# Projections first as block products, then values with attention, in a hybrid decoder layer

## The chip, the core and the metric

The kernel runs on one core of one Trainium2 chip. The time is the device time of one execution in microseconds (us), and the number compared is the median of several runs. The core has a matrix engine (PE in the profile), a vector engine (DVE), a scalar engine (ACT), a general engine (POOL), and a sync engine (SP), which in this kernel issues the DMA transfers. Each engine works through its own instructions in program order, and waits on semaphores for the others.

## What is computed

```python
h = x * (1 + scale) + shift                      # scale, shift, gate = silu(c) @ w_ada + b_ada
proj = h @ w_in                                  # q k v | g_attn | u B C g_conv | m_attn m_conv
# attention: 3 groups of 4 heads of 128; (window, dilation) = (128,1), (512,4), (2048,16)
s = q . k * 128**-0.5 + bias(distance), causal, window only
o_g = softmax(s) @ v;   lse_g = log of the softmax denominator
o = sum over the 3 groups of softmax(lse)_g * o_g
a_out = (o * silu(g_attn)) @ w_attn_out
# short convolution
z = C * u;  y_conv = conv3_causal(z)
s_out = (B * y_conv * silu(g_conv)) @ w_conv_out
merged = sigmoid(m_attn) * a_out + sigmoid(m_conv) * s_out
out = LayerNorm(alpha * x + (1 + gate) * (merged @ w_o))
```

There are 2048 tokens and 1024 channels, all in float32. To keep the precision, each factor of a big product is split into a rounded part and a remainder ("hi" and "lo"): ScalarE casts the rounded part, VectorE subtracts it to get the remainder, and TensorE runs three matmuls (hi by hi, hi by lo, lo by hi) for each product. Every weight and every activation that goes into such a product costs these two operations.

## The kernel before

Tokens are cut into four chunks of 512. The program has three stages.

The *start* (L180 to L257) computes scale and shift on VectorE while h arrives, and runs the first six query and key units on TensorE as the channels of h arrive. It also builds the twelve bias tables `nb` that attention adds to the scores.

The *attention stage* (L156 to L591) is a list of segments, run by `run_segs` (L156). A segment is one weight unit: a query unit (`qseg`), a key unit (`kseg`), a pair of value units (`vseg`), or a unit of g_attn (`aseg`). A query, key or g_attn unit is a plain product (`gemm`, L140 to L142): 8 channel tiles by 3 matmuls of 128x512, so 24 matmuls. A pair of value units is 4 blocks of 24 matmuls of 128x256 (L186 to L188). The weights of a unit are loaded five segments ahead and split three segments ahead (`wlo`, L103). The parts of attention of a head (scores, transposes, products with the values) are put behind later segments with `after`, so that they alternate with projections. First come the four chunks with groups 1 and 2 (up to about 752 us), whose outputs and softmax statistics go to DRAM (`o_scr`, `st_scr`). Then come the four chunks with group 0 (752 to 1202 us): there `done` (L525 to L557) sends the last statistics through DRAM, works out the weights of the three groups in `al`, writes them to `al_scr`; and `merge` (L559 to L577) loads them broadcast (`ab`), loads the outputs of groups 1 and 2 (`og`), adds the three, and multiplies with silu(g_attn) (`gt`).

The *block products* come last (from L594). Two halves of the tokens and two weights at a time form a product of 2 by 2 blocks, which `products` (L678 to L680) computes with seven block products instead of eight: seven pairs of sums of the blocks (the T rows of the activations, `t_row`: seven splits and four subtractions a row, four rows; and the parts of the weights, `stationary_parts`), then 84 matmuls of 128x512 a step, then sums on VectorE. The stage runs u with C, g_conv with B, m_attn with m_conv (24 steps for each half of the tokens), then the attention output (`w_ao`), the convolution output (`w_co`) for each half, and `w_o` with the LayerNorm.

The places that the prediction speaks of are `gemm` with its users, the merge, `prep` (which loads x, modulates it and splits h for a chunk), and the T rows that each stage of block products begins with.

Of the kernel before, what the change touches and what calls it, by code (L numbers as in the profile page):

```python
# [17 lines left out]
P = 128  # L18
# [5 lines left out]
NH = 4  # L24
# [29 lines left out]
@with_exitstack  # L54
def layer_kernel(ctx: ExitStack, tc: tile.TileContext, x, xm, xn, cvec, wada, bada, w_main, w_v,
                 convw, convb, relb, onehot, w_ao, w_co, w_o, ln_g, ln_b, out):
# [3 lines left out]
    dram = ctx.enter_context(tc.tile_pool(name="dram", bufs=1, space=bass.MemoryType.DRAM))  # L60
    const = ctx.enter_context(tc.tile_pool(name="const", bufs=1))
    stage = ExitStack()
    wp = stage.enter_context(tc.tile_pool(name="wp", bufs=3))
    hp = stage.enter_context(tc.tile_pool(name="hp", bufs=1))
    psum1 = stage.enter_context(tc.tile_pool(name="psum", bufs=1, space=bass.MemoryType.PSUM))

    def bank(tag, bufs):
        return psum1.tile([P, CH], F32, tag=tag, bufs=bufs, name=tag)


    ident = const.tile([P, P], F32, name="ident")
    make_identity(nc, ident)

    def bcast_row(src, n):
        return bass.AP(tensor=src.tensor, offset=src.offset, ap=[[0, P], [1, n]])

    mod = const.tile([P, 3, KT], F32, name="mod")
    badat = const.tile([P, 3, KT], F32, name="badat")
    scp = const.tile([P, KT], F32, name="scp")
    cw = const.tile([P, KT, 4], F32, name="cw")  # L80
    powe = const.tile([P, 1], F32, name="powe")
    halo = const.tile([P, KT, 2], F32, name="halo")


    lagd = dram.tile([3, NH, LAG], F32, name="lagd")
    o_scr = dram.tile([2, NH, NCH, NCH, P, P], F32, name="o_scr")
    st_scr = dram.tile([2, NCH, NH, 4, 2, NCH, 32], F32, name="st_scr")
    st0_scr = dram.tile([NCH, 2, NH * 4, P], F32, name="st0_scr")
    al_scr = dram.tile([NCH, 3, NH * 4, P], F32, name="al_scr")
    om_scr = dram.tile([NCH, P, NH, CH], F32, name="om_scr")  # L90
    y_scr = dram.tile([2, KT, P, 2 * CH], F32, name="y_scr")
    sg_scr = dram.tile([2, 2, KT, P, 2 * CH], F32, name="sg_scr")
    pa_scr = dram.tile([2, KT, P, 2 * CH], F32, name="pa_scr")
    mg_scr = dram.tile([SEQ // P, P, KT, P], F32, name="mg_scr")

    kq = stage.enter_context(tc.tile_pool(name="kq", bufs=1, reuse_waits="tile"))
    nb = [[kq.tile([P, 256 if g < 2 else P], F32, name=f"nb{g}{j}") for j in range(NH)]
          for g in range(3)]


    def split(hi, lo, src):
        S.copy(hi, src)  # L102
        V.tensor_sub(lo, src, hi.bitcast(F32))  # L103
# [6 lines left out]
    def split_unit(raw):  # L110
        hi = wp.tile([P, DM], F32R, name="whi", bufs=3)
        lo = wp.tile([P, DM], F32R, name="wlo", bufs=3)
        split(hi, lo, raw)
        return hi, lo

    def h_pair():
        return (hp.tile([P, CH], F32R, name="hhi", bufs=9), hp.tile([P, CH], F32R, name="hlo", bufs=9))

    def load_x(src, k):
        xs = hp.tile([P, CH], F32, name="xs", bufs=3)  # L120
        SP.dma_start(xs, src[:, k, :])
        return xs

    def modulate(E, xs, k):
        E.tensor_scalar(xs, xs, scp[:, k:k + 1], mod[:, 0, k:k + 1], op0=ALU.mult, op1=ALU.add)
        hi, lo = h_pair()
        split(hi, lo, xs)
        return hi, lo

    def prep(src, store):  # L130
        def pre():
            for k in range(KT):
                store.append(modulate(V, load_x(src, k), k))
        return pre

    def gemm_k(ps, unit, xk, k, n, base=0):
        hi, lo = unit
        xh, xl = xk
        sl = slice((base + k) * P, (base + k + 1) * P)
        PE.matmul(ps, hi[:, sl], xh, start=k == 0, stop=False)  # L140
        PE.matmul(ps, hi[:, sl], xl, start=False, stop=False)  # L141
        PE.matmul(ps, lo[:, sl], xh, start=False, stop=k == n - 1)  # L142

    def gemm(unit, rhs, base=0):
        ps = bank("mm", 3)
        for k, xk in enumerate(rhs):
            gemm_k(ps, unit, xk, k, len(rhs), base)
        return ps
# [35 lines left out]
    def pass3(o, a, b, start, stop):  # L184
# [5 lines left out]
    halos = [(kq.tile([P, P], F32R, name=f"halo_h{j}"), kq.tile([P, P], F32R, name=f"halo_l{j}"))  # L190
             for j in range(NH)]

    def evac_q(g, ps):
        qh = kq.tile([P, CH], F32R, name="qh", bufs=3)
        if g == 2:
            q = qh.bitcast(F32)
            S.activation(classes(q), classes_of(ps), AF.Copy, scale=-QSCALE)
            return q
        ql = kq.tile([P, CH], F32R, name="ql", bufs=3)
        S.activation(qh, ps, AF.Copy, scale=-QSCALE)  # L200
        V.scalar_tensor_tensor(ql, ps, -QSCALE, qh.bitcast(F32), op0=ALU.mult, op1=ALU.subtract)
        return qh, ql

    def evac_k(g, ps, j, c):

        kh = kq.tile([P, P + CH], F32R, name="kh", bufs=3)
        if g == 2:
            k = kh[:, P:].bitcast(F32)
            S.copy(classes(k), classes_of(ps))
            return k  # L210
        kl = kq.tile([P, P + CH], F32R, name="kl", bufs=3)
        split(kh[:, P:], kl[:, P:], ps)
        if g == 0:
            for t, hl in ((kh, halos[j][0]), (kl, halos[j][1])):
                if c > 0:
                    G.tensor_copy(t[:, :P], hl.bitcast(F32))
                if c < NCH - 1:
                    G.tensor_copy(hl, t[:, CH:].bitcast(F32))
        return kh, kl

# [5 lines left out]


    def silu_c(cb, sg):
        SP.dma_start(cb, bcast_row(cvec, DM))
        S.activation(sg, cb, AF.Sigmoid)  # L230
        V.tensor_mul(cb, cb, sg)

    def dot_v(wt, cb, junk, acc):
        for q in range(4):
            sl = slice(q * 256, (q + 1) * 256)
            V.tensor_tensor_reduce(junk, wt[:, sl], cb[:, sl], 1.0, 0.0, ALU.mult, ALU.add,
                                   accum_out=acc[:, q:q + 1])

    def dot_end(m, k, acc):
        V.tensor_reduce(mod[:, m, k:k + 1], acc, axis=AX.X, op=ALU.add)  # L240
        V.tensor_add(mod[:, m, k:k + 1], mod[:, m, k:k + 1], badat[:, m, k:k + 1])

    first_h, first_heads = [], {}
    first_units = [W_Q + NH, W_K + NH, W_Q + NH + 1, W_K + NH + 1, W_Q + NH + 2, W_K + NH + 2]
    with tc.tile_pool(name="ada", bufs=1) as ada:
        cb = ada.tile([P, DM], F32, name="cb")
        silu_c(cb, ada.tile([P, DM], F32, name="prod", bufs=2))
        SP.dma_start(badat, bada)
        flip = ada.tile([P, P], F32, name="flip")
# [783 lines left out]
```

## Time and profile before

| what | us |
|---|---|
| median of 3 runs | 2729.73 (2729.53 to 2733.96) |
| the profiled execution, its own time | 2724.08 |
| its span in the trace | 2722.3 |
| TensorE busy in the span | 2518.6 (93%) |
| VectorE busy | 1684.8 (62%) |
| ScalarE busy | 1002.0 (37%) |
| mean granted clock, as a share of full speed | 0.969 |

The span is the time from the first to the last instruction of the trace. The time of the execution is 1.78 us longer. Busy times are sums over the span, so they say nothing about where an engine waits; for this the rows below go by stretches of the program: start (0 to 100 us), attention with groups 1 and 2 (to 752), with group 0 (to 1202), the last merge (to 1238), the block products of the projections (to 2200), a hand-over, and the output products with the LayerNorm (to 2722).

### The profile page before, as it was taken

To read this page: it belongs to the slowest core of one execution; us is meant where nothing else is said; L and a number is where in the kernel's file an instruction comes from. 1 tells how busy PE (TensorE), PEld (TensorE's weight loads), DVE (VectorE), ACT (ScalarE), POOL (GpSimd) and SP (SyncE) were. 2 spreads that over 40 slices of the span, in tenths; PEclk is the share of its full clock that TensorE was granted. 3 is DMA by queue.
4 is the path that set the end of the run, shared out by engine and by line. 5 is a ranking of instruction groups with operands and counts; after the bars stand their busy time and mean duration, and the time that the engine had idled before them with its cause. 6 is when DMAs were issued, how large, how long until landed. Compare 5 with 4: busy or idle time off the path is not lost.

```text
span 2722.3 us, 31895 instructions
## 1 busy us (share of the span) xinstructions
PE 2518.6 (93%) x12070; PEld 2114.6 (78%) x12070; DVE 1684.8 (62%) x2800; ACT 1002.0 (37%) x1675; POOL 142.3 (5%) x126
## 2 busy tenths in 40 slices
PE   6999999999999999965999999899999988988886
PEld 4898998989988888853888888688888856666665
DVE  8334334243255676747776765777665568788887
ACT  4223333232343434425333343633333343343332
POOL 2000000000000000000000000000000000113123
PEclk9999999999999999986999999999999989998998
DMA  7223233232233553614221233422213247657343
GB/s 261 78 87 116 85 102 108 64 120 78 87 126 100 175 162 122 184 56 162 78 70 62 70 129 135 139 78 70 70 62 116 101 152 266 206 195 238 113 140 104
DMA packets 160302, 331.25 MB, mean 122 GB/s; under 512 B 18727, under 2 KB 70003, under 8 KB 160148
## 3 DMA queue, kind: packets, MB, share of 16 engines
q1 hardware_dynamic: 160148, 329.21, 36.8%
q8 instruction: 94, 1.54, 0.2%
q14 instruction: 60, 0.49, 0.1%
HBM read 265.93 MB, written 63.23 MB: 121 GB/s over the span
## 4 chain that ended last, share of the span: by engine, by line
PE 72%; DVE 12%; DMA 8%; issue 4%; ACT 2%; POOL 1%; SPq 0%; POOLq 0%; DVEq 0%; ACTq 0%
PE pb L678 12%; PE pb L679 12%; PE pb L680 12%; PE mm L140 6%; PE mm L141 6%; PE mm L142 6%; PE mm L188 4%; PE mm L186 4%; PE mm L187 4%; DVE tl L103 2%; DMA og<-o_scr 1%; PE pt L367 1%; DVE w2l L103 1%; DMA xs<-in_xn 1%; DVE hlo L103 1%
## 5 line engine op out<-in xcount | busy, mean ns | idle before, releaser
L678 PE MATMUL pb<-th,w2h 128*128 128x512 f32 x1632 | 650.2, 403 | 105.5 <-ACT th L102 91.3
L679 PE MATMUL pb<-tl,w2h 128*128 128x512 f32 x1632 | 648.2, 399 | 10.9 <-DVE tl L103 10.9
L680 PE MATMUL pb<-th,w2l 128*128 128x512 f32 x1632 | 640.4, 396 | 1.0 <-DVE w2l L103 1.0
L678 PEld LDWEIGHTS pb<-th,w2h 128*128 128x128 f32 x1632 | 312.5, 192 | 201.4 <-ACT th L102 114.8
L103 DVE TENSOR_TENSOR wlo<-raw,whi 128x1024 fp32r<-128x1024 f32 x155 | 189.7, 1224 | 419.3 <-ACT whi L102 410.3
L679 PEld LDWEIGHTS pb<-tl,w2h 128*128 128x128 f32 x1632 | 312.9, 192 | 87.5 <-DVE tl L103 23.9
L680 PEld LDWEIGHTS pb<-th,w2l 128*128 128x128 f32 x1632 | 313.0, 192 | 67.0 <-DVE w2l L103 2.6
L140 PE MATMUL mm<-hhi,whi 128*128 128x512 f32 x856 | 343.0, 401 | 21.2 <-ACT hhi L102 21.2
L142 PE MATMUL mm<-hhi,wlo 128*128 128x512 f32 x856 | 336.2, 393 | 3.9 <-DVE wlo L103 3.9
L141 PE MATMUL mm<-hlo,whi 128*128 128x512 f32 x856 | 336.3, 393 | 1.7 <-DVE hlo L103 1.7
L102 ACT CAST whi<-raw 128x1024 fp32r<-128x1024 f32 x155 | 162.6, 1049 | 446.0 <-issue 184.4
L186 PE MATMUL mm<-whi,hhi 128*128 128x256 f32 x768 | 246.0, 322 | 4.5 <-ACT hhi L102 4.4
L188 PE MATMUL mm<-whi,hlo 128*128 128x256 f32 x768 | 244.8, 323 | 2.0 <-DVE hlo L103 1.8
L187 PE MATMUL mm<-wlo,hhi 128*128 128x256 f32 x768 | 244.5, 321 | 0.0
L102 ACT CAST w2h<-raw 128x1024 fp32r<-128x1024 f32 (+1 forms) x136 | 139.6, 1027 | 275.0 <-PE pb L679 262.0
L103 DVE TENSOR_TENSOR w2l<-raw,w2h 128x1024 fp32r<-128x1024 f32 (+1 forms) x136 | 169.1, 1244 | 110.4 <-ACT w2h L102 110.3
L684 ACT COPY t<-pb 128x512 f32<-128x512 f32 x216 | 125.0, 582 | 232.6 <-PE pb L680 221.3
L140 PEld LDWEIGHTS mm<-hhi,whi 128*128 128x128 f32 x856 | 162.4, 190 | 53.8 <-ACT hhi L102 23.2
L142 PEld LDWEIGHTS mm<-hhi,wlo 128*128 128x128 f32 x856 | 162.1, 189 | 39.4 <-DVE wlo L103 5.0
L186 PEld LDWEIGHTS mm<-whi,hhi 128*128 128x128 f32 x768 | 182.0, 237 | 8.8 <-ACT hhi L102 7.1
L141 PEld LDWEIGHTS mm<-hlo,whi 128*128 128x128 f32 x856 | 162.5, 190 | 33.7 <-DVE hlo L103 2.9
L188 PEld LDWEIGHTS mm<-whi,hlo 128*128 128x128 f32 x768 | 181.2, 237 | 4.7 <-DVE hlo L103 4.0
(197 smaller groups left out, 3513.1 us busy)
## 6 DMA issues: line engine op xcount, KB each, us to landing
raw<-in_w_main SPq DMA_DIRECT2D x208, 512.0 KB
raw<-in_w_v SPq DMA_DIRECT2D x48, 512.0 KB
sg_scr<-big SPq DMA_DIRECT2D x32, 512.0 KB
big<-sg_scr SPq DMA_DIRECT2D x32, 512.0 KB
ab<-al_scr SPq DMA_DIRECT2D x48, 256.0 KB
wt<-in_wada SPq DMA_DIRECT2D x16, 512.0 KB
xs<-in_xm SPq DMA_DIRECT2D x32, 256.0 KB
o_scr<-o SPq DMA_DIRECT2D x32, 256.0 KB
```

Of the source, the lines that this page charges most:

```text
L102: S.copy(hi, src)
L103: V.tensor_sub(lo, src, hi.bitcast(F32))
L140: PE.matmul(ps, hi[:, sl], xh, start=k == 0, stop=False)
L141: PE.matmul(ps, hi[:, sl], xl, start=False, stop=False)
L142: PE.matmul(ps, lo[:, sl], xh, start=False, stop=k == n - 1)
L186: PE.matmul(o, a[0], b[0], start=start, stop=False)
L187: PE.matmul(o, a[0], b[1], start=False, stop=False)
L188: PE.matmul(o, a[1], b[0], start=False, stop=stop)
L678: PE.matmul(bank, hi[:, sl], th, start=first, stop=False, **kw)
L679: PE.matmul(bank, hi[:, sl], tl, start=False, stop=False, **kw)
L680: PE.matmul(bank, lo[:, sl], th, start=False, stop=n == len(rows) - 1, **kw)
L684: S.copy(r, bank)
```

## The change

The query, key and g_attn projections leave the attention stage. They become steps of the block products, and all block products of projections now come first in the program; then attention with only the value projections; then the outputs. In detail:

- The start modulates h straight into T rows of the first half. Its first step (queries of group 1) runs row by row in seven banks (`products_by_row`).
- Queries and keys are 12 steps a half, g_attn 2 steps a half, in place of 24 + 4 plain units for each of four chunks. The results go to `qk_scr` and (as silu) to `ga_scr` in DRAM. For groups 1 and 2 the last sums are written with a stride, in the order of the tokens of a dilated group.
- The bias tables are made between the steps and kept in `nb_scr`; attention loads them back.
- The attention stage has segments of two blocks of values (48 matmuls of 128x256). Queries and keys of a head are loaded from `qk_scr` (`load_qk`) two segments before they are used, cast and split.
- The merge loads `gt` from `ga_scr`, ready for the multiplication.
- The outputs run in the order co of half 0, ao of both halves, co of half 1, w_o.

The core of the diff:

```diff
-                def qseg(i, unit, box=box):
-                    box["q"] = evac_q(g, gemm(unit, h))
-                def kseg(i, unit, j=j, box=box):
-                    attend(i, j, box["q"], evac_k(g, gemm(unit, h), j, c))
-                seg([w_main[W_Q + g * NH + j]], qseg)
-                seg([w_main[W_K + g * NH + j]], kseg)
+    def load_qk(g, j, c, box):
+        n0 = P if g == 0 and c > 0 else 0
+        qr = kq.tile([P, CH], F32, name="qr", bufs=2)
+        kr = kq.tile([P, P + CH], F32, name="kr", bufs=2)
+        SP.dma_start(qr, qk_scr[g * NH + j, :, c * CH:(c + 1) * CH])
+        SP.dma_start(kr[:, P - n0:], qk_scr[12 + g * NH + j, :, c * CH - n0:(c + 1) * CH])
...
+        S.activation(qh, qr, AF.Copy, scale=-QSCALE)
+        V.scalar_tensor_tensor(ql, qr, -QSCALE, qh.bitcast(F32), op0=ALU.mult, op1=ALU.subtract)
+        split(kh[:, P - n0:], kl[:, P - n0:], kr[:, P - n0:])
...
-        after(i + 1, qk)
-        d = 0 if g == 0 and j == NH - 1 else 1
-        after(i + 2 + d, tr)
-        after(i + 3 + d, pv)
+        after(i, qk)
+        after(i + 1, tr)
+        after(i + 2, pv)
...
+            for b0 in (0, 2):
+                i = len(segs)
+                seg([w_v[g, pair, 0], w_v[g, pair, 1]] if b0 == 0 else [],
+                    lambda i, *units, b0=b0, vseg=vseg: vseg(i, *units, b0=b0))
+            for n in range(2):
+                j, at = 2 * pair + n, i + 1 + n
+                qk_box = {}
+                after(at - 2, lambda j=j, qk_box=qk_box: load_qk(g, j, c, qk_box))
...
-            S.activation(ab, gt[j], AF.Sigmoid)
-            V.tensor_mul(gt[j], gt[j], ab)
-            V.tensor_mul(o0[j], o0[j], gt[j])
+            gt = pm.tile([P, CH], F32, name="gt", bufs=2)
+            SP.dma_start(gt, ga_scr[j, :, c * CH:(c + 1) * CH])
+            V.tensor_mul(o0[j], o0[j], gt)
...
-            def aseg(i, unit, h=h, j=j, gt=gt, merge=merge):
-                ps = gemm(unit, h)
+            order = [u + g * NH + j for g in (1, 2, 0) for u in (W_Q, W_K) for j in (0, 2)]
+            for u in order:
+                            if local:
+                                V.tensor_add(m[k][:, at * CH:(at + 1) * CH], r, bank)
+                            else:
+                                V.tensor_add(m[k].rearrange("q (c n a) -> q c n a", c=4, n=2)[:, :, at],
+                                             r.rearrange("q (a c) -> q c a", c=4),
+                                             bank.rearrange("q (a c) -> q c a", c=4))
...
+                if p == 0 and u == W_Q + NH:
+                    todo.append(lambda heads=heads, T=T: products_by_row(S0, T, range(4), *heads()))
+                else:
+                    step(w, w_main[u], w_main[u + 1], CH, use, pre)
+            for j in range(0, NH, 2):
+                def silus(j=j, p=p):
+                            V.tensor_add(o, r, bank)
+                            S.activation(s, o, AF.Sigmoid)
+                            V.tensor_mul(o, o, s)
```

Three places show how instructions move.

SP, the merge of the second chunk of group 0, before. The names are the DRAM buffers of the group weights (`al_scr`), of the outputs of groups 1 and 2 (`o_scr`), of the merged output (`om_scr`), and the weights of the next chunk (`in_w_v`, `in_w_main`).

```order
L557 DMA al_scr<-al 16x3x128
L564 DMA ab<-al_scr 128x512 x3
L107 DMA raw<-in_w_v 128x1024
L564 DMA ab<-al_scr 128x512
L107 DMA raw<-in_w_v 128x1024
L564 DMA ab<-al_scr 128x512
L570 DMA og<-o_scr 128x4x128 x2
L564 DMA ab<-al_scr 128x512
L107 DMA raw<-in_w_main 128x1024
L577 DMA om_scr<-o_7946 128x512
```

The same place after:

```order
L144 DMA kr<-qk_scr 128x640
L392 DMA al_scr<-al 16x3x128
L143 DMA qr<-qk_scr 128x512
L144 DMA kr<-qk_scr 128x640
L399 DMA ab<-al_scr 128x512 x4
L143 DMA qr<-qk_scr 128x512
L399 DMA ab<-al_scr 128x512
L405 DMA og<-o_scr 128x4x128
L399 DMA ab<-al_scr 128x512
L405 DMA og<-o_scr 128x4x128
L399 DMA ab<-al_scr 128x512
L412 DMA om_scr<-o_16116 128x512
```

The weight loads between the broadcasts are gone from this stretch, and loads of queries and keys (`qr`, `kr`) stand in the queue among the loads of the merge.

DVE, the same merge, before (`wlo` is the remainder of a weight unit, `ql` and `kl` those of queries and keys, `o` a head's output, `ab` a broadcast weight, `og` the output of another group):

```order
L103 TENSOR_TENSOR wlo<-raw,whi 128x1024
L103 TENSOR_TENSOR vb<-mm,va 128x256
L567 TENSOR_TENSOR o_7946<-o_7946,ab 128x512
L103 TENSOR_TENSOR wlo<-raw,whi 128x1024
L572 TENSOR_TENSOR ab<-ab,og 128x4x128 x2
L573 TENSOR_TENSOR o_7946<-o_7946,ab 128x512
L103 TENSOR_TENSOR wlo<-raw,whi 128x1024
L573 TENSOR_TENSOR o_7946<-o_7946,ab 128x512
L575 TENSOR_TENSOR gt_8154<-gt_8154,ab 128x512
L201 SCALAR_TENSOR_TENSOR ql<-mm,qh 128x512
L576 TENSOR_TENSOR o_7946<-o_7946,gt_8154 128x512
```

The same merge after (`p,st` are scores with bias and their row statistics):

```order
L156 SCALAR_TENSOR_TENSOR ql<-qr,qh 128x512
L467 TENSOR_TENSOR kl<-kr,kh 128x640
L467 TENSOR_TENSOR vb<-mm,va 128x512
L402 TENSOR_TENSOR o_16116<-o_16116,ab 128x512
L407 TENSOR_TENSOR ab<-ab,og 128x4x128
L194 ISA p,st<-s,nb_10796 128x256
L194 ISA st 128x1
L408 TENSOR_TENSOR o_16116<-o_16116,ab 128x512
L407 TENSOR_TENSOR ab<-ab,og 128x4x128
L402 TENSOR_TENSOR o_16259<-o_16259,ab 128x512
L408 TENSOR_TENSOR o_16116<-o_16116,ab 128x512
L194 ISA p,st<-s,nb_10796 128x256
```

Weight splits stood between the steps of the merge; now scores of the next heads stand there, and `ql` and `kl` are made from loaded tiles (`qr`, `kr`) instead of banks.

DVE, the end of attention, before (`rows` are the statistics of the last head, `al` and `nm` the group weights):

```order
L525 COPY o_10428<-ot 128x512
L471 COPY rows<-pt 32x128
L585 COPY gt_10486<-mm 128x512
L546 TENSOR_TENSOR nm<-al 16x128
L547 TENSOR_TENSOR nm<-nm,al 16x128
L549 TENSOR_TENSOR al<-nm,al 16x128 x3
L551 TENSOR_TENSOR al<-al 16x384
L552 TENSOR_TENSOR nm<-al 16x128
L553 TENSOR_TENSOR nm<-nm,al 16x128
L554 RECIPROCAL nm<-nm 16x128
L556 TENSOR_TENSOR al<-al,nm 16x128 x3
L567 TENSOR_TENSOR o_10076<-o_10076,ab 128x512
```

The same place after (`w2l`, `xs`, `w1l` belong to the first weights of co):

```order
L360 COPY o_17535<-ot 128x512
L467 TENSOR_TENSOR w2l<-raw,w2h 128x1024
L549 TENSOR_TENSOR xs<-raw 128x512
L381 TENSOR_TENSOR nm<-al 16x128
L550 TENSOR_TENSOR xs<-xs,raw 128x512
L382 TENSOR_TENSOR nm<-nm,al 16x128
L554 TENSOR_TENSOR raw<-raw 128x512
L384 TENSOR_TENSOR al<-nm,al 16x128 x3
L467 TENSOR_TENSOR w2l<-xs,w2h 128x1024
L467 TENSOR_TENSOR w2l<-raw,w2h 128x1024
L386 TENSOR_TENSOR al<-al 16x384
```

The weight preparation of the next block products now stands between the steps of the group weights; before, it came behind the merge.

## Rows read from the trace of the kernel before

**Rows 1.** The page: busy time with share, and the chain that ended last.

```profile
PE 2518.6 (93%) x12070; PEld 2114.6 (78%) x12070; DVE 1684.8 (62%) x2800; ACT 1002.0 (37%) x1675; POOL 142.3 (5%) x126
...
PE 72%; DVE 12%; DMA 8%; issue 4%; ACT 2%; POOL 1%; SPq 0%; POOLq 0%; DVEq 0%; ACTq 0%
```

**Rows 2.** Windows by stage: stretch, length, busy us of each engine, clock, DMA.

```profile
core 0: us, PE busy (x) PEld busy (x) DVE busy (x) ACT busy (x) POOL busy (x), PEclk, DMA share, GB/s
0.00:60.00 60.00, 35.71 (x128) 25.73 (x129) 51.63 (x146) 24.50 (x66) 16.52 (x14) 1.00 0.76 274
60.00:100.00 40.00, 36.00 (x248) 31.80 (x247) 20.12 (x35) 10.25 (x18) 0.00 (x0) 1.00 0.42 114
392.00:572.00 180.00, 179.62 (x978) 163.38 (x977) 66.91 (x142) 60.23 (x134) 0.00 (x0) 1.00 0.30 94
752.00:1202.00 450.00, 434.78 (x2504) 380.99 (x2502) 278.45 (x538) 176.95 (x350) 25.49 (x48) 0.98 0.42 132
977.00:1087.00 110.00, 107.13 (x616) 93.96 (x615) 75.76 (x142) 45.24 (x86) 7.77 (x19) 0.98 0.50 156
1202.00:1238.00 36.00, 0.00 (x0) 0.00 (x0) 25.34 (x41) 4.32 (x6) 0.00 (x0) 0.57 0.54 154
1238.00:1290.00 52.00, 32.47 (x99) 21.22 (x100) 42.83 (x65) 32.87 (x46) 0.00 (x0) 0.71 0.50 167
1290.00:1710.00 420.00, 420.00 (x1852) 347.23 (x1851) 285.46 (x430) 155.72 (x188) 0.00 (x0) 1.00 0.27 92
2200.00:2240.00 40.00, 28.52 (x72) 16.52 (x72) 31.38 (x54) 18.19 (x32) 0.00 (x0) 0.70 0.46 151
2240.00:2722.30 482.30, 402.05 (x1614) 307.42 (x1613) 395.39 (x566) 168.99 (x244) 100.29 (x64) 0.93 0.53 181
```

**Rows 3.** Timeline of TensorE: start, duration, engine, line, operation.

```profile
419.10 0.48 PE L140 MATMUL mm<-hhi,whi 128*128 128x512 f32 x1
...
424.65 0.60 PE L367 MATMUL pt<-ident,p 128*128 128x128 f32 x4
...
438.46 0.28 PE L186 MATMUL mm<-whi,hhi 128*128 128x256 f32 x1
...
449.98 0.49 PE L367 MATMUL pt<-ident,p 128*128 128x128 f32 x3
```

**Rows 4.** Groups of VectorE by form, 977 to 1087 us (one chunk of group 0).

```profile
L103 DVE TENSOR_TENSOR wlo<-raw,whi 128x1024 fp32r<-128x1024 f32 x16 | 19.6, 1224 | 15.6 <-ACT whi L102 15.6
...
L575 DVE TENSOR_TENSOR gt<-gt,ab 128x512 f32<-128x512 f32 x4 | 2.9, 726 | 0.0
...
L585 DVE COPY gt<-mm 128x512 f32<-128x512 f32 x4 | 2.8, 689 | 9.7 <-PE mm L142 9.7
```

**Rows 5.** Timeline of VectorE, back to back, in the block products.

```profile
1250.56 1.22 DVE L103 TENSOR_TENSOR w2l<-raw,w2h 128x1024 fp32r<-128x1024 f32 x1
1251.70 0.68 DVE L103 TENSOR_TENSOR w1l<-t,w1h 128x512 fp32r<-128x512 f32 x1
1252.30 0.68 DVE L626 TENSOR_TENSOR t<-big,t 128x512 f32<-128x512 f32 x1
```

**Rows 6.** Timeline of VectorE, end of attention; in brackets what ended an idle time.

```profile
1196.84 0.27 DVE L471 COPY rows<-pt 32x128 f32<-32x128 f32 x1
...
1212.37 0.69 DVE L567 TENSOR_TENSOR o<-o,ab 128x512 f32<-128x512 f32 x1 [5.20 <-DMA ab<-al_scr]
...
1237.26 0.69 DVE L576 TENSOR_TENSOR o<-o,gt 128x512 f32<-128x512 f32 x1
```

**Rows 7.** Windows of 10 us around the hand-over to the block products.

```profile
1210.00:1220.00 10.00, 0.00 (x0) 0.00 (x0) 6.29 (x9) 2.54 (x3) 0.00 (x0) 0.50 0.68 184
1250.00:1260.00 10.00, 6.93 (x13) 4.14 (x14) 10.00 (x16) 10.00 (x16) 0.00 (x0) 0.50 0.66 231
```

**Rows 8.** Groups of VectorE by form, 392 to 572 us: copies without and with stride.

```profile
L486 DVE COPY o<-ot 128x512 f32<-128x512 f32 x4 | 4.2, 1054 | 0.0
...
L484 DVE COPY o<-ot 128x512 f32<-128x512 f32 x4 | 2.7, 682 | 0.0
```

More of the change, by code (lines that the diff above doesn't have):

```diff
@@ L92, in layer_kernel @@
[L92 to L103, printed above, removed]
@@ L132, in pre @@
             for k in range(KT):
-                store.append(modulate(V, load_x(src, k), k))
-        return pre
[L136 to L148, printed above, removed]
+                xs = hp.tile([P, CH], F32, name="xs", bufs=3)
+                SP.dma_start(xs, src[:, k, :])
+                V.tensor_scalar(xs, xs, scp[:, k:k + 1], mod[:, 0, k:k + 1], op0=ALU.mult, op1=ALU.add)
+                hi = hp.tile([P, CH], F32R, name="hhi", bufs=9)
+                lo = hp.tile([P, CH], F32R, name="hlo", bufs=9)
+                split(hi, lo, xs)
+                store.append((hi, lo))
+        return pre
     segs = []
@@ L328, in attention @@
+    def attention(i, g, j, c, box, v, voff, vprev, st, done):
         P_t, keys, PT = [None] * 4, [None] * 4, {}
@@ L472, in stats_out, with pre_all, pre @@
         write(rows)
+    def pre_all(first, src, h, g):
+        make = prep(src, h)
+        def pre():
+            if g is not None:
+                load_nb(g)
+            make()
+        segs[first][2] = pre
     for c in range(NCH):
[L476 removed]
+        h = []
         first = len(segs)
@@ new lines, in bias_rows @@
+    def bias_rows():
+        rb, flip = const.tile([N_BUCKETS + 1, 3 * NH], F32, name="rb"), row()[:, :P]
+        V.memset(rb, 1.0)
+        SP.dma_start(rb[:N_BUCKETS], relb)
+        for g in range(3):
+            oh, lg = half(), half()
+            SP.dma_start(oh[:N_BUCKETS + 1, :LAG], onehot[:, g])
+            pl = ps_bank()
+            PE.matmul(pl[:NH, :LAG], rb[:, g * NH:(g + 1) * NH], oh[:N_BUCKETS + 1, :LAG], start=True, stop=True)
+            S.copy(lg[:NH, :LAG], pl[:NH, :LAG])
+            SP.dma_start(lagd[g], lg[:NH, :LAG])
+        G.memset(flip, 0.0)
+        G.affine_select(out=flip, in_=flip, compare_op=ALU.not_equal, fill=1.0, base=1 - P,
+                        pattern=[[1, P]], channel_multiplier=1)
+        return flip
@@ L919, in layer_kernel @@
+        step(w, w_ao[d // 2], None, 256,
+             [(T, range(2 * p, 2 * p + 2), gated(0, p, d, p == 0)) for p in range(2)], pre)
+        pre = None
+    co(1, True)
     T, rows_ = {}, {}
```

726 lines of the change are left out of this document (366 added, 360 removed).

## The prediction

> **What bounds the kernel now.** The page comes first: TensorE is busy for 93% of the span, and it holds 72% of the chain that ended last, VectorE 12% [rows 1]. That is an average, so the windows by stage come next [rows 2]. With groups 1 and 2 (392 to 572 us stands for 100 to 752) TensorE is busy for 179.62 of 180 us and VectorE for 66.91: matmuls alone set the time. A chunk of group 0 (977 to 1087) has 107.13 of 110 us on TensorE and 75.76 on VectorE, so vector work is hidden there, though it is not small. The block products are full (420.00 of 420 us). TensorE is not the bound in four places: the start, the last merge (1202 to 1238: none), the ramp behind it (32.47 of 52), and the outputs (402.05 of 482.3, with VectorE at 395.39). So removing matmuls pays where TensorE is full, until VectorE or a transfer is the next limit. I read that limit stage by stage.
>
> **1. Matmuls.** A query unit runs from 419.10 to 424.65, and the next work starts at its end: 24 matmuls in 5.55 us, units elsewhere 5.47 to 5.55, mean 5.53 [rows 3]. Removed: 28 units in each of 4 chunks, 112 x 5.53 = 619 us. Added: (12 + 2) steps in each of 2 halves, 28 x 84 matmuls. The block products run 1852 matmuls in 420 us, 0.2268 us each [rows 2], so 28 x 84 x 0.2268 = 533 us. Difference: **-86 us**. These steps stay bound by TensorE: a step is 19.05 us, while VectorE needs 6.4 us for the parts of the weights (three 1024 wide at 1.14, five 512 wide at 0.60, the spacing of back-to-back starts [rows 5]) and some eight sums, about 11.2 us in all.
>
> **2. Start.** Before, the first 60 us hold 128 matmuls of 0.231 us, 30 us of work; to 100 us TensorE is busy for 36.00, of which I count 31 as work that both kernels have (the rest makes the bias tables). So 100 us hold some 61 us of work: a loss of 39 to 40. VectorE is the bound there, 51.63 of 60 us [rows 2]. After, its first stretch loses 8 modulations of 0.46, 8 remainders of 0.60 and 6 unit splits of 1.14, 15.3 us, and gains the first weights (6.4), the T rows (4 rows x 11 operations x 0.60 = 26.4) and the next step's first split (1.7). 51.6 - 15.3 + 34.5 = 70.8, with the 8.4 us that VectorE is idle there now, 79 us. The first step is done at about 82 us with 19 us of work: a loss of 63. The step that runs row by row is already taken in. +23; if the T rows hide the idle time +12, if each row waits once more for its transfer +35. The small matmuls of the bias tables stand between steps, in float32 and dependent on transfers: +5 (2 to 10). **+28 us.**
>
> **3. Hand-over to attention.** It waits for the last gate's sigmoid and store, then 12 loads of bias tables, x, weights, modulation and splits, some 24 us by the spacing of these operations. Before, there was one hand-over here that goes: from the block products to the output of attention, 2200 to 2240 us with 72 matmuls, 40 - 72 x 0.2268 = 23.7 us lost [rows 2]. **0** (-10 to +15).
>
> **4. Groups 1 and 2.** Per chunk 16 units go, 180 - 88.5 = 91.5 us of TensorE remain; VectorE keeps 66.91 - 16 x 1.14 = 48.7 us, which fits beside it. What is new is a wait: the loads of a head's queries and keys are issued two segments (some 11 to 23 us) ahead on SP, and queued behind them, or ahead of them, stand the stores of outputs and the loads of weights. ScalarE's and VectorE's casts queue behind a late load, then TensorE's scores. No row of before has this load. The nearest is the broadcast that the merge waits 5.20 us for [rows 6]. Two segments cover it, so the low end is 0; at the high end 3 of these 5.20 us show at each of 32 heads, 96 us. I take **+15**, near the covered end.
>
> **5. Group 0 and the last merge** (752 to 1238, 486 us). 12 units of each chunk go, 4 x 12 x 5.53 = 265, counted in step 1; 221 us would be left. But VectorE works 278.45 + 25.34 there [rows 2], and loses only 12 splits of 1.14 (16 in a chunk now, with four for the values [rows 4]) and eight 512-wide operations of 0.60 on `gt` [rows 4]: 18.5 us a chunk, 74 in all. 303.8 - 74 = 230 us remain on VectorE, against some 40 us a chunk on TensorE: values 2 x 11.5 (96 matmuls from 438.46 to 449.98 [rows 3]) and scores, transposes and products 107.13 - 12 x 5.53 - 23 = 17.8 [rows 2]. So VectorE becomes the bound of this stage. It won't be full, since scores, exponentials and transposes go back and forth between three engines. Where it was the bound, in the outputs, it was busy for 395.39 of 482.3 us, 82% [rows 2]. 230 / 0.82 = 280: **+60 us** over the 221. At the low end 0: it is packed at once. At the high end +100: each chunk also shows the chain from the last statistics to the merge (1196.84 to 1212.37 [rows 6], 15.5 us), which today other matmuls hide in all but the last chunk. I take the row that has the same bound.
>
> **6. Ramp behind attention.** Before, 52 us with 99 matmuls; the T rows of the next product are the same 26.4 us, and still behind the merge in VectorE's order. Only its first weights (6.4 us) move ahead of the merge: **-6**.
>
> Sum against the span: 2722.3 - 86 + 28 + 0 + 15 + 60 - 6 = 2733; the execution is 1.78 us longer than its span, and the median of the runs 5.65 us above the profiled execution (2729.73 against 2724.08), so 2740 us, 0.4% above the median before.
>
> **The rivals.** *Faster: the vector work of group 0 packs.* The merges and the modulation of the next chunk give VectorE other work while it waits for scores; a window of the ramp has it at 10.00 of 10 us [rows 7]. At 95% the 230 us become 242 (+21 for +60), and the loads of step 4 are covered: 2740 - 39 - 15 = 2686. Against it: in the outputs there is other work too, and it reaches 82%.
>
> *TensorE's clock falls in group 0.* With no matmuls, the granted clock is 0.50 (1210 to 1220), and it is still 0.50 while the ramp has 6.93 us of TensorE in 10 (1250 to 1260) [rows 7]: 1.2 GHz in place of 2.4. If TensorE waits for VectorE through group 0, its 40 us a chunk become 80, above the 70 of step 5: 4 x 10 = +40, 2780. Against it: 752 to 1202 has 0.98 [rows 2], with TensorE at 97%. It decides from the point where TensorE's work at the low clock is longer than VectorE's.
> The Trainium skill ("TensorE: Matmul & The Clock Gate", section "HAM oscillation — how this bites in real kernels") says that a loop whose bursts of matmuls are shorter than the wait for their operands starts each burst at the low clock. The waits there are for DMA, while here they would be for VectorE; no row of this stage shows such bursts yet.
>
> *Late loads.* The high end of step 4, 32 x 3 = 96 in place of 15: 2821. For it: SP issues in order, and each load has a store ahead of it that waits for VectorE.
>
> *It does not do what it says:* the sums of queries and keys of groups 1 and 2 are written with a stride, and the copy of that kind takes 1054 ns, a plain one 682 [rows 8]. 16 steps x 4 sums x 0.37 = 24 us if all of it showed: 2764. Against it: VectorE has 8 us to spare in a step.
> The Trainium skill ("SBUF — State Buffer", section "Door 1: The DMA port swizzle (why `[64,N]` ≈ `[32,N]`)") has 16-byte lines, of which an access wants at least two hits for full bandwidth, so that four-byte elements four apart pay for each; the two copies agree with that, by a factor of 1.55.
>
> **How the numbers follow.** The forecast has 0.47, with its own range of 2715 to 2765 (step 2 from +17 to +45, step 5 from +40 to +80); the vector work packs 0.25; the clock 0.15; late loads 0.10; the stride 0.03. A measurement of this kernel tells 0.2%, 5.5 us, from no change: below 2724 is faster, above 2735 slower. Of the forecast's 0.47, 0.08 lie below, 0.15 between, 0.24 above. Faster 0.25 + 0.08 = 0.33, same 0.15, slower 0.24 + 0.15 + 0.10 + 0.03 = 0.52. The range reaches down to the packed case and up past the clock, 2685 to 2805; late loads in full and a packing better than 95% are left out.
>
> **What would show it.** Step 1: the block products at 0.227 us a matmul for 76 steps. Step 2: first sums at about 82 us. Step 4: idle time of VectorE or ScalarE ended by `qr` or `kr`. Step 5: a stage of group 0 of some 280 us with VectorE above 80% and TensorE waiting for it; a granted clock near 1 there or, by the second rival, at 0.5. I am wrong if the stage of group 0 is near 240 us, if attention with groups 1 and 2 takes much more than 92 us a chunk, or if query and key steps take longer than 19 us.

## The result and the profile after

The changed kernel takes 2763.87 us (median of 4 runs, 2760.77 to 2765.38) against 2729.63 us of the kernel before: a ratio of 1.0124, 95% interval 1.0105 to 1.0143, 34 us slower. The forecast was 2740 in a range of 2685 to 2805, slower with a chance of 0.52.

The page of the profiled execution (busy us with share, and the chain that ended last) answers to [rows 1]:

```profile
PE 2478.2 (90%) x11734; PEld 2086.0 (76%) x11734; DVE 1821.2 (66%) x2996; ACT 1059.2 (38%) x1763; POOL 117.2 (4%) x78
...
PE 70%; DVE 11%; DMA 8%; issue 5%; ACT 3%; POOL 1%; SPq 1%; POOLq 0%; DVEq 0%; ACTq 0%
```

TensorE is busy for 40 us less and waits for 77 us more: its busy time fell from 2518.6 to 2478.2 while the span rose from 2722.3 to 2759.0. Busy time fell by less than the 86 us of matmuls removed; the mean granted clock is 0.944 in place of 0.969, and matmuls that run at the low clock take longer (0.43 us from start to start in place of 0.23, shown below). Where the waits are, the windows by stage tell (columns as in [rows 2]); they are the first 100 us, the bias tables, projections, the first two chunks of groups 1 and 2, group 0 up to its last values, its end with the ramp, and the outputs:

```profile
0.00:100.00 100.00, 58.53 (x184) 40.47 (x185) 88.56 (x205) 52.31 (x104) 16.69 (x14) 0.88 0.58 195
100.00:302.00 202.00, 184.69 (x773) 148.94 (x773) 97.07 (x111) 53.62 (x78) 0.00 (x0) 0.94 0.34 110
302.00:800.00 498.00, 498.00 (x2198) 412.35 (x2197) 327.66 (x483) 182.25 (x223) 0.00 (x0) 1.00 0.28 93
...
1573.42:1668.00 94.58, 90.66 (x538) 89.27 (x539) 46.59 (x106) 47.84 (x99) 0.00 (x0) 0.96 0.52 157
1668.00:1765.00 97.00, 96.04 (x617) 94.59 (x616) 51.43 (x139) 51.86 (x126) 0.00 (x0) 1.00 0.46 136
...
1944.00:2113.00 169.00, 152.93 (x1180) 149.11 (x1178) 140.19 (x338) 94.32 (x234) 0.00 (x0) 0.92 0.60 178
2113.00:2262.00 149.00, 58.69 (x253) 47.10 (x252) 122.16 (x227) 40.54 (x87) 0.00 (x0) 0.66 0.66 200
...
2262.40:2759.00 496.60, 411.63 (x1606) 312.38 (x1604) 391.30 (x574) 167.81 (x246) 100.47 (x64) 0.90 0.52 175
```

Three things are to be seen. The new projection steps are full (2198 matmuls in 498 us, 0.2266 each), but for those from 100 to 302 us. In group 0 VectorE is the busiest in the last part (122.16 of 149) and TensorE waits. The outputs, which were not full before either (400.14 of 480.4 us), take 16 us longer.

The table is the whole account. Its boundaries are starts of matmuls in the timelines of TensorE: a value block's first one for attention (758.0 before, 1573.4 and 1943.6 after), and every 84th for the block products, so that a step is the distance of two starts (19.0 us where nothing waits).

| stretch | before, us | after, us | change | forecast |
|---|---|---|---|---|
| matmuls: 112 units out, 28 steps in | 619 | 533 | -86 | -86 |
| first steps, lost | 38.2 (218.2 - 180, its first chunk of attention) | 58.4 (115.6 - 3 x 19.05) | +20 | +23 |
| bias tables, lost | in the 38.2 | 33.5 (147.8 - 6 x 19.05) | +33.5 | +5 |
| hand-over (ao before, attention after) | 24 | 16.7 | -7 | 0 |
| groups 1 and 2, four chunks without queries and keys | 366 | 370.2 | +4 | +15 |
| group 0 and ramp, without queries, keys, g_attn | 528.7 - 265.4 = 263.3 | 318.8 | +55.5 | +54 |
| outputs behind the ramp | 480.4 | 496.6 | +16 | 0 |
| sum | | | +36 | +11 |

Of the measured spans the difference is 36.7.

The row of group 0 and the ramp joins two forecasts, steps 5 and 6. The last step of the last merge parts them; these are the stretches up to it and behind it, before and after:

```profile
758.00:1238.00 480.00, 428.78 (x2474) 375.97 (x2472) 299.23 (x565) 177.72 (x344) 25.49 (x48) 0.95 0.43 133
1238.00:1286.70 48.70, 29.17 (x85) 18.65 (x86) 40.37 (x62) 31.34 (x44) 0.00 (x0) 0.69 0.52 174
...
1943.60:2236.50 292.90, 189.90 (x1353) 180.94 (x1351) 238.39 (x527) 124.52 (x304) 0.00 (x0) 0.78 0.64 189
2236.50:2262.40 25.90, 22.52 (x83) 15.98 (x84) 24.76 (x40) 10.37 (x17) 0.00 (x0) 0.93 0.51 172
```

The stage grew by 292.9 - (480.0 - 265.4) = 78 us, and the ramp shrank by 23.

Three waits carry what is not in the forecast or needs a cause. They are read from the view of waits (engine, line, what it waited for: us in all, times, longest). First, 150 to 302 us of the changed kernel:

```profile
PE pb L714 <- DMA t<-lagd: 14.2, 3, 6.1
...
PE pb L696 <- DMA t<-in_onehot: 3.1, 2, 1.9
```

TensorE stands before the small matmuls that turn lag rows into bias tables (L714) until their loads land. The longest two, 6.1 and 5.8 us, are for the second pair of loads of a group. Behind such a wait the matmuls are slower: in TensorE's timeline (start, duration, operation) they start 0.43 us apart behind the last of the three, and 0.23 some four us later.

```profile
282.08 0.63 PE L567 MATMUL pb<-tl,w2h 128*128 128x512 f32 x1
282.50 0.63 PE L568 MATMUL pb<-th,w2l 128*128 128x512 f32 x1
...
286.14 0.40 PE L567 MATMUL pb<-tl,w2h 128*128 128x512 f32 x1
286.37 0.39 PE L568 MATMUL pb<-th,w2l 128*128 128x512 f32 x1
```

Second, group 0 with its end, 1944 to 2262 us:

```profile
ACT pth L466 <- PE ot L123: 34.7, 5, 17.3
PE ot L121 <- DVE o L360: 34.0, 7, 17.2
ACT th L466 <- DMA big<-y_scr: 33.8, 3, 31.0
...
PE pb L567 <- DVE tl L467: 31.5, 2, 31.3
```

TensorE waits for VectorE: 34.0 us for the copy that empties the bank of a head's output, and 31.5 for the T rows behind the merge. Before, from 758 to 1238 us, its longest wait in all was this:

```profile
PE s L187 <- DVE kl L103: 7.4, 4, 4.0
```

The longest of the seven waits for the copy, in VectorE's own timeline (start, duration, operation, in brackets what ended an idle time):

```profile
2156.76 0.41 DVE L375 COPY al<-alr 16x128 f32<-16x128 f32 x2 [0.21 <-DMA al_scr<-al]
...
2160.61 0.69 DVE L402 TENSOR_TENSOR o<-o,ab 128x512 f32<-128x512 f32 x1 [3.18 <-DMA ab<-al_scr]
2162.53 1.06 DVE L407 TENSOR_TENSOR ab<-ab,og 128x512 f32<-128x512 f32 x1 [1.23 <-DMA ab<-al_scr]
...
2171.59 0.69 DVE L411 TENSOR_TENSOR o<-o,gt 128x512 f32<-128x512 f32 x1
2172.22 0.69 DVE L360 COPY o<-ot 128x512 f32<-128x512 f32 x1
```

The copy stands behind the merge of two heads of the chunk before, and the merge behind its broadcasts. Before, TensorE had matmuls of other projections in this place. Third, the attention output (ao), 2364 to 2441 us:

```profile
POOL big L943 <- DMA t<-pa_scr: 45.6, 5, 12.9
...
ACT t L575 <- POOL big L943: 13.7, 2, 8.7
PE pb L566 <- ACT t L575: 11.2, 4, 6.9
```

In the new order of outputs ao adds what co left in DRAM (L943), and the chain of waits runs from this load over POOL and ScalarE to TensorE. This is a part of the 16 us. By the steps, ao's last three take 76.2 us in place of 63.2, while those of co's first half, which no longer adds, save 6. Another 12 us lie in the first step behind the ramp that starts with new T rows, co's before and ao's after:

```profile
2305.30:2337.90 32.60, 26.20 (x86) 16.20 (x85) 31.71 (x52) 18.31 (x31) 0.00 (x0) 0.90 0.56 192
...
2320.40:2365.30 44.90, 32.70 (x86) 19.83 (x85) 34.88 (x59) 17.54 (x31) 4.15 (x3) 0.70 0.51 164
```

In ao's, TensorE waits 9.7 us for ScalarE's casts of the T rows, and those 8.9 us for the loads of the merged outputs.

### The profile page after: what moved, and what is told of

Same layout as the page of the kernel before. It is cut to its first block, busy times and chain, and to the rows that moved or that the text cites. A ratio compares the mean times of both kernels' runs of the same rounds, so it can differ in the third digit from the quotient of the medians.

```text
span 2759.0 us, 31825 instructions
## 1 busy us (share of the span) xinstructions
PE 2478.2 (90%) x11734; PEld 2086.0 (76%) x11734; DVE 1821.2 (66%) x2996; ACT 1059.2 (38%) x1763; POOL 117.2 (4%) x78
## 4 chain that ended last, share of the span: by engine, by line
PE 70%; DVE 11%; DMA 8%; issue 5%; ACT 3%; POOL 1%; SPq 1%; POOLq 0%; DVEq 0%; ACTq 0%
PE pb L566 19%; PE pb L567 19%; PE pb L568 19%; PE mm L123 3%; PE mm L121 3%; PE mm L122 3%; DVE tl L467 2%; DMA og<-o_scr 1%; PE pt L203 1%; DMA xs<-in_xn 1%; DMA ab<-al_scr 1%; DVE w2l L467 1%; DVE ab L407 1%; DMA raw<-mg_scr 1%; DVE o L408 0%
## 5 line engine op out<-in xcount | busy, mean ns | idle before, releaser
L566 PE MATMUL pb<-th,w2h 128*128 128x512 f32 x2304 | 918.6, 402 | 98.9 <-ACT th L466 74.0
L567 PE MATMUL pb<-tl,w2h 128*128 128x512 f32 x2304 | 916.2, 399 | 45.4 <-DVE tl L467 45.3
L568 PE MATMUL pb<-th,w2l 128*128 128x512 f32 x2304 | 907.9, 397 | 2.6 <-DVE w2l L467 2.6
L566 PEld LDWEIGHTS pb<-th,w2h 128*128 128x128 f32 x2304 | 441.8, 192 | 223.4 <-ACT th L466 96.0
L567 PEld LDWEIGHTS pb<-tl,w2h 128*128 128x128 f32 x2304 | 442.9, 192 | 148.3 <-DVE tl L467 57.4
L568 PEld LDWEIGHTS pb<-th,w2l 128*128 128x128 f32 x2304 | 442.9, 192 | 96.8 <-DVE w2l L467 4.9
L121 PE MATMUL mm<-whi,hhi 128*128 128x256 f32 x768 | 253.4, 331 | 28.5 <-ACT hhi L466 28.4
L122 PEld LDWEIGHTS mm<-wlo,hhi 128*128 128x128 f32 x768 | 186.1, 243 | 2.4 <-DVE wlo L467 2.3
L566 PE MATMUL pb<-th,w1h 128*128 128x512 f32 x384 | 154.2, 402 | 18.1 <-DVE big L1008 10.1
L567 PE MATMUL pb<-tl,w1h 128*128 128x512 f32 x384 | 152.2, 396 | 0.0
L568 PE MATMUL pb<-th,w1l 128*128 128x512 f32 x384 | 151.8, 395 | 0.0
L943 POOL TENSOR_TENSOR big<-big,t 128x512 f32<-128x512 f32 x32 | 47.7, 1498 | 2437.2 <-DMA t<-pa_scr 2390.2
```

The source lines that it names most:

```text
L121: PE.matmul(o, a[0], b[0], start=start, stop=False)
L122: PE.matmul(o, a[0], b[1], start=False, stop=False)
L566: PE.matmul(bank, a[0], b[0], start=start, stop=False, **kw)
L567: PE.matmul(bank, a[0], b[1], start=False, stop=False, **kw)
L568: PE.matmul(bank, a[1], b[0], start=False, stop=stop, **kw)
L943: G.tensor_add(o, o, a_)
```

## The experiments

Medians are in us; the kernel before had 2728.7 to 2731.9 in these sets. The changed kernel was timed in another set (2763.87, with the kernel before at 2729.63), so "us less" carries some 3 us between sets. Stage lengths come from one profile each, from the first value block of group 0 to the second step of the outputs (318.8 in the changed kernel; 320.3 and 318.2 in the two whose edits lie elsewhere, bias_ahead and qk_one_ahead), unless another stretch is named.

**Bias loads one step ahead.** The loads of a group's four rows go into one tile ahead of the step, in place of two and two just ahead of their matmuls.

```diff
+        for j in range(NH):
+            t = lagd[g, j]
+            SP.dma_start(hks[0][:, j * 256:j * 256 + w],
+                         bass.AP(tensor=t.tensor, offset=t.offset + 256 - w, ap=[[1, P], [1, w]]))
...
+                    if p == 0 and u in (W_Q, W_Q + 2, W_K):
+                        bias_loads((W_Q, W_Q + 2, W_K).index(u))
                     step(w, w_main[u], w_main[u + 1], CH, use, pre)
```

> Changed kernel, but the loads of a group's four lag rows are issued one step ahead of the small matmuls that use them. Stall theory: in the changed kernel the six steps from 153.7 to 301.6 us take 147.8 us in place of 6 x 19.05 = 114.3, because TensorE waits 14.2 us in all for these loads in its own order, and runs slower for a while behind each wait (granted clock 0.90 to 0.93). Without the waits the six steps take 120 to 128 us and the run is 18 to 27 us shorter, near 2741. Rival: the small float32 matmuls themselves (11 us busy) and their banks cost the time; then the run is less than 8 us shorter.

2741.51, ratio to before 1.0036 (1.0023 to 1.0049): 22 us less. The window of the same 202 us:

```profile
100.00:302.00 202.00, 198.53 (x868) 161.91 (x867) 108.38 (x124) 61.73 (x88) 0.00 (x0) 0.99 0.38 124
```

868 matmuls in place of 773, and a granted clock of 0.99 in place of 0.94. No wait for `lagd` is left. So the stall is shown, and its price is larger than the 14.2 us of the wait itself: most of the rest are the slower matmuls behind each wait, which are gone too. The six steps take 126.1 us; of the 12 still lost, 6 are in the first of them, which makes the lag rows and waits for `in_onehot`, and 6 in the others.

**Copies of outputs on ScalarE.**

```diff
-            V.tensor_copy(o0[j], ps)
+            S.copy(o0[j], ps)
```

> Changed kernel, but the copy of a head's output of group 0 out of its bank is made by ScalarE instead of VectorE. Order theory: in the stage of group 0 TensorE waits 34 us in all for these copies, which stand in VectorE's order behind merges that wait for broadcasts; the waits go and the stage is 15 to 30 us shorter. Amount theory: only VectorE's amount of work counts; 16 copies of 0.60 us at 82% are 12 us, so 8 to 12 us shorter. Clock theory: TensorE's low clock (0.83 there) sets the stage; under 5 us.

2750.03, ratio 1.0066 (1.0049 to 1.0083): 14 us less, above the amount theory and just under the order theory. Its waits refute the order theory as it was put:

```profile
PE ot L121 <- ACT o L360: 39.5, 9, 18.2
...
ACT o L360 <- DMA om_scr<-o: 30.7, 7, 15.3
```

The wait for the copies did not go; it is 39.5 us. Now the copy waits for its buffer, which the merge of the chunk before frees with its store. The stage is 312.7, 6 us shorter in the profile, which is of the slowest of the four runs (2756.78).

**The same with six shared buffers.**

```diff
-            o0[j] = pm.tile([P, CH], F32, name=f"o0{j}")
+            o0[j] = pm.tile([P, CH], F32, name="o0", bufs=6)
...
-                    pt = pa.tile([P, 256], F32, name="p", bufs=10)
+                    pt = pa.tile([P, 256], F32, name="p", bufs=8)
```

> Changed kernel with the copies of group 0's outputs on ScalarE, and in place of one buffer a head six that all heads share (the score tiles go from ten to eight to make room). Buffer theory, formed on the run with the copies on ScalarE alone: there TensorE still waited 39.5 us for the copies, and ScalarE 30.7 us for the store of the merged output of the chunk before, which frees the buffer; with six buffers this wait is under 10 us, TensorE's for the copies under 15, and the run is 12 to 30 us shorter than with the copies on ScalarE alone (2750), 2720 to 2738. Amount theory: VectorE's work is the same as there, so 2745 to 2755.

2747.22, ratio 1.0071 (1.0054 to 1.0088): no different from the run before it. The buffer theory falls, in the time and in both waits:

```profile
PE pb L566 <- ACT th L466: 57.8, 2, 56.1
...
ACT o L360 <- DMA om_scr<-o: 29.0, 4, 12.3
...
PE ot L121 <- ACT o L360: 17.7, 2, 12.4
```

ScalarE still waits 29.0 us for the store, and TensorE's wait for the copies halved, 39.5 to 17.7, while the one at the end, for the T rows of the outputs, is 57.8 in all. The T rows stand behind the merges on VectorE, so TensorE reaches its end earlier and waits there. The stage is 310.6, 8 us shorter.

**Modulation of x on ScalarE in group 0.**

```diff
+                if on_scalar:
+                    S.activation(xs, xs, AF.Identity, scale=scp[:, k:k + 1], bias=mod[:, 0, k:k + 1])
+                else:
                     V.tensor_scalar(xs, xs, scp[:, k:k + 1], mod[:, 0, k:k + 1], op0=ALU.mult, op1=ALU.add)
```

> Changed kernel, but ScalarE instead of VectorE modulates x in the stage of group 0 (32 operations of 512). Amount theory: VectorE loses 32 x 0.46 = 14.7 us of 189.5 us of work, at 82% busy: 14 to 18 us shorter. Order theory: the operations that TensorE waits for are the copies behind the merges, which keep their place; 0 to 8 us shorter. Clock theory: within 4 us.

2746.82, ratio 1.0062 (1.0045 to 1.0079): 17 us less, as the amount theory had it. By the profile only 11 of that lie in the stage, between the two theories:

```profile
1943.20:2251.30 308.10, 206.96 (x1435) 191.99 (x1434) 252.01 (x539) 152.19 (x349) 0.00 (x0) 0.83 0.66 195
```

The stage is 308.1, 10.7 us shorter, and VectorE is busy in it for 252.0 us in place of 263.2, 11.1 less. Another 3 us are in the outputs, which this edit doesn't touch. (The outputs behind the ramp took 493.8 to 497.7 us in eight profiles with the changed kernel's order, so differences of a few us in one profile tell nothing.)

The three runs so far that take work from VectorE here, and the first combination below, read alike: VectorE is busy for 254.5 us of a stage of 312.7 (copies on ScalarE), 255.2 of 310.6 (with six buffers), 252.0 of 308.1 and 243.7 of 301.3 (combination), each 81 to 82%, where the changed kernel has 263.2 of 318.8, 83%.

**Filler on TensorE in group 0.** Half a block of matmuls more ahead of each block of values; the real ones overwrite them.

```diff
+                    for k in range(KT // 2 if g == 0 else 0):
+                        hi, lo = box["u"][k // 4]
+                        sl = slice((k % 4) * 256, (k % 4 + 1) * 256)
+                        pass3(o, [h_block(t, b) for t in h[k]], (hi[:, sl], lo[:, sl]), k == 0, k == KT // 2 - 1)
```

> Changed kernel, but each block of values of group 0 is preceded by half a block of matmuls more into the same bank, which the real ones overwrite: 4 x 2 x 48 = 384 matmuls of 128x256, 46 us at full clock, on TensorE alone. Theory that VectorE and its order bound the stage: the extra work goes mostly into waits of TensorE, 0 to 20 us longer. Clock theory: with TensorE less idle its clock stays up, and the stage is no longer or shorter, -20 to 0. Theory that TensorE bounds the stage in spite of its waits: 40 us longer or more.

2773.49, ratio 1.0156 (1.0137 to 1.0175): 10 us more. In the profile, up to the last values and behind them:

```profile
1938.30:2147.20 208.90, 197.42 (x1603) 195.46 (x1602) 163.36 (x374) 97.78 (x239) 0.00 (x0) 0.97 0.59 174
2147.20:2272.40 125.20, 47.95 (x220) 37.03 (x219) 100.70 (x193) 37.97 (x82) 0.00 (x0) 0.67 0.64 189
```

The stage took 334.1 us, 15 more, and what is ahead of it 5 less in this profile, where the code is the same. TensorE got 46 us more of work and the clock rose to 0.97 up to the last values, where the changed kernel has 0.92; the stage did not get shorter, so the clock theory falls as it was put. What the low clock costs here stays open: TensorE's busy time in the stage rose by 33 us (212.4 to 245.4) and not by 46, so the work that was there became some 13 us cheaper. TensorE doesn't bound the stage alone either, since two thirds of the 46 us were hidden. They were hidden at the end: up to the last values the stage is 39 us longer (208.9 in place of 169.6), behind them 24 shorter (125.2 in place of 149.2), where VectorE has 100.7 us of work left in place of 122.4. With the run before this reads as one picture: a chain that goes back and forth between the engines, in which VectorE's work counts nearly in full (10.7 us for 11.1) and TensorE's about a third (15 for 46).

**Queries and keys loaded one segment ahead.**

```diff
-                after(at - 2, lambda j=j, qk_box=qk_box: load_qk(g, j, c, qk_box))
+                after(at - 1, lambda j=j, qk_box=qk_box: load_qk(g, j, c, qk_box))
```

> Changed kernel with the loads of a head's queries and keys issued one segment ahead instead of two. Theory that the loads are covered with room (groups 1 and 2 take 92.4 us a chunk, where the matmuls alone need 91.5): a segment is some 11.5 us there, the load lands in about 5, so 0 to 8 us longer. Rival of the prediction, late loads: each of 32 heads of groups 1 and 2 shows 3 us or more, 60 to 100 us longer.

2758.69, ratio 1.0111 (1.0094 to 1.0128): not longer. The four chunks of groups 1 and 2 take 370.2 us, as with two segments. The loads are covered even by one segment, and the rival of late loads falls.

**The attention output first.**

```diff
-    co(0, False)
...
-             [(T, range(2 * p, 2 * p + 2), gated(0, p, d, p == 0)) for p in range(2)], pre)
+             [(T, range(2 * p, 2 * p + 2), gated(0, p, d, False)) for p in range(2)], pre)
...
+    co(0, True)
     co(1, True)
```

> Changed kernel with the order of outputs that the kernel before has: attention output (ao) first, then both halves of the convolution output (co), which both add. Theory that the order costs the 15 us of the outputs: ao's steps fall from 121 us in all to about 106, but its T rows wait for the last merge's stores (some 5 us each way); 2750 to 2760 where the changed kernel has 2764. Rival, the order pays for itself: the T rows of ao behind the merge cost as much or more; 2764 to 2785.

2753.52, ratio 1.0086 (1.0072 to 1.0101): 10 us less, as the first theory had it. The window of the outputs behind the ramp, of this kernel and of the kernel before:

```profile
2269.80:2750.20 480.40, 401.83 (x1605) 307.15 (x1603) 392.46 (x563) 169.09 (x244) 99.66 (x64) 0.93 0.54 181
```

```profile
2241.90:2722.30 480.40, 400.14 (x1606) 305.88 (x1604) 393.63 (x563) 168.99 (x244) 100.29 (x64) 0.93 0.54 181
```

With the old order the stretch is as long as before, 480.4 us in both, so the 16 us of the table are the order's (13 to 17, by the profiles with the new order). Some 9 us come back ahead of it: the stage from group 0 to the second step is 328 in place of 318.8, since the T rows of ao wait for the merged outputs through DRAM.

**Combinations.**

> Changed kernel with the bias loads ahead, x of group 0 modulated by ScalarE, and the copies of group 0's outputs on ScalarE with six shared buffers. If the gains add: 2763.9 - 22 - 17 - 14 = 2711, less what the buffers bring, 2690 to 2711, below the kernel before. If the edits in group 0 take the same waits, or ScalarE becomes the bound there: 2720 to 2735.

2726.12, ratio 0.9992 (0.998 to 1.0005), level with the kernel before. The stage is 301.3, 17.5 us shorter, which is about the sum of 8.2 and 10.7 in the profiles; it was the sum of the medians that promised too much.

> Changed kernel with the bias loads ahead, x of group 0 modulated by ScalarE, and the attention output before both convolution outputs. Each alone took 22, 17 and 10 us from 2764. If they add: 2708 to 2722, below the kernel before. If the second and third wait for the same thing at the end of attention (the combination of the first two with ScalarE's copies stayed 13 us above the sum of its parts): 2722 to 2735, no different from before.

2724.73, ratio 0.997 (0.9958 to 0.9982), 0.3% faster than the kernel before, but 39 us below 2764 and not the 49 of the medians. It lies in the second range; the reason given there doesn't show. The stage is 318.1, and the second and third edit alone had changed it by -10.7 and +9.2, which adds up to 317.3. Again the single medians promised more than the stretches that the edits touch.

On top of these three, the first steps row by row:

```diff
-                    step(w, w_main[u], w_main[u + 1], CH, use, pre)
+                    step(w, w_main[u], w_main[u + 1], CH, use, pre, products_by_row if pre else None)
...
-             CH, [(T, range(4), norm)], pre)
+             CH, [(T, range(4), norm)], pre, products_by_row if pre else None)
```

(The same for `step` with `w_co`.)

> The kernel three_edits, in which the first step behind each set of T rows (second half of the projections, both convolution outputs, w_o) runs row by row in seven banks, as the changed kernel's very first step does, so that TensorE starts on a row while VectorE prepares the next. If the T rows, a wait of TensorE of 11 to 25 us at each of these four places, are what remains: 5 to 12 us less at each, 20 to 45 us below three_edits, 2670 to 2700. Rival: VectorE's T rows bound these places and the first step is hidden only in part, since the last row ends when it did: under 10 us below three_edits.

2721.52, ratio 0.9965 (0.9951 to 0.9979): the fastest here, but only 3 us below three_edits, within the intervals of both. The rival was right. In the first half of co the first step shrank from 31.8 to 27.3 us, and the second grew from 19.3 to 23.1. VectorE, which prepares T rows and the next weights, is busy for 94% of both (25.55 of 27.20 and 21.78 of 23.10 us).

## Why the prediction was right, and where it was not

*What bounds the kernel, and step 1* held: 19.0 us a step, -86 us.

*Step 2* was right in its first half: 58.4 us lost in the first steps, where the working had 63. It failed in its second half. "The small matmuls of the bias tables stand between steps, in float32 and dependent on transfers: +5 (2 to 10)" was the largest miss, 33.5 us. The sentence names the dependence and then prices only the matmuls. The second pair of loads of a group is issued on SP behind the stores of the first pair, so in the first two groups it shows a full round trip on TensorE's path, 6.1 and 5.8 us (2.2 in the third). Moving the loads alone took back 22 us. [rows 6] had the price of such a round trip, 5.20 us, at hand.

*Step 3* was 7 us too high, *step 4* 11 us: four chunks took 370.2 us, the matmuls alone need 366, and one segment of lead is still enough (qk_one_ahead).

*Steps 5 and 6* came out as forecast only together, +55.5 against +54. Step 5 by itself was +78 in place of +60, step 6 -23 in place of -6. The two misses are one: VectorE did some 16 us of work for the next product (weights and half of the T rows' subtractions) ahead of the last merge's end, which lengthens the stage and shortens the ramp. Step 6 took 6.4 us out of the ramp for it, and step 5 added none. The share is the one taken over from [rows 2]: 238.4 of 292.9 us, 81%, and over the stage with its ramp it stayed at 81 to 82% in the four runs that took work from VectorE. So the mechanism held: VectorE bounds the stage, at a share of about 82% that stands for the back and forth. Why this stage and the outputs, which do other work, have the same share, no run shows. VectorE is not the only bound: up to the last values work on TensorE counts too (filler_g0). The high end, +100, is not quite its own sum: three more chains of 15.5 us on +60 are +106.

*The outputs:* the sum had no term for the new order of the outputs. It cost 16 us behind the ramp and saved 9 ahead of it (ao_first). This was not read at all in the prediction. In the new order the addition, with its load and its POOL operation, falls on the first half of ao, whose steps have eight sums where those of co have four; and ao's T rows, which before were a part of the hand-over, now stand between two products. By the lengths of the steps these are some 7 and 12 us, with 3 less in the second half of co; no run parts them.

*The rivals.* The packed case (0.25) did not come. The clock fell, to 0.66 at the end of group 0 and 0.92 ahead of it, but TensorE was busy for 189.9 us up to the last merge, where the second rival had 4 x 80 and the forecast 4 x 40; at the end TensorE waits anyway (58.69 of 149 us busy). The Trainium skill ("TensorE: Matmul & The Clock Gate", section "HAM oscillation — how this bites in real kernels") has bursts of matmuls that are shorter than the wait for their operands start at the low clock. The trace agrees in sign at the end of group 0, clock 0.66, though the waits are for VectorE. That the clock alone sets this stage's time filler_g0 refutes; that it costs nothing there it doesn't show. The low clock did cost time at the bias tables, where TensorE was the bound: clock 0.94 over 202 us, 0.99 without the waits. The stride had its price on VectorE: a sum whose two inputs are read four elements apart (it is they, in the code, and not the result that have the stride) takes 1.08 us, a plain one 0.69. In the view of a line, min, median and max are in ns:

```profile
L787 DVE TENSOR_TENSOR big<-t,pb x64: 1045/1076/1100, 80.2 to 985.5; 128x512 f32<-128x512 f32 x64
...
L785 DVE TENSOR_TENSOR big<-t,pb x32: 686/689/689, 234.4 to 1061.7; 128x512 f32<-128x512 f32 x32
```

These 25 us were hidden: in the second half, where the first eight steps have such sums, they take 19.0 us from the fourth on, as the plain ones behind them do. That the rival's 2764 is the measured time is chance.

So the sign is right, though by a chance of 0.52 the prediction hardly leaned on it, and the main term too. The 24 us between 2740 and 2764 are the bias tables (+28.5) and the order of outputs (+16), less what steps 3 and 4 had too much (18), and a few us between a profiled execution and the median. That the time lies in the forecast's own range, 2715 to 2765, is owed to misses that cancel in part; without what steps 3 and 4 had too much it would be some 2782.

What stays open: which part of the back and forth in group 0 could be taken out by another order of VectorE's queue (copies of the next head ahead of the merge) was not tried, and neither was what the low clock costs there.

## What to carry to other kernels

When matmuls are removed from a stage, price what they covered: here 86 us of matmuls went in all, and 55 came back in the one stage where VectorE had been busy for 62% of the time behind them. The busy share of a stage that already has the new bound was a better estimate than either end of the range, and it held in four more runs. Add up edits by the stretches that they touch, not by single medians. Price a small helper by its round trips on the path, not by its operations: the bias tables cost nearly two steps of 84 matmuls, and loading one step earlier gave 22 us back.

## What the hardware showed that was not expected

A wait of 6 us on TensorE cost more than itself: three waits of 14.2 us in all fall into two stretches of 50 us with a granted clock of 0.93 and 0.90 (200 to 250 and 250 to 300), matmuls behind them start 0.43 us apart in place of 0.23, and taking the waits away gave 22 us. A sum of 128x512 with both inputs read four elements apart took VectorE 1.08 us in place of 0.69. What the low clock costs in group 0 no run shows by itself.
